# Where the added row of the first LayerNorm joins the residual: in the input stage, or on w_out's token tiles

## The chip, the cores and the metric

One core of one Trainium2 chip runs the whole kernel. The metric is the time of the execution on the device in microseconds. Three runs of the kernel before took 1259.07, 1259.10 and 1259.88 us; the median is 1259.1.

## What is computed

A decoder layer over 1024 tokens of width 1024, with 16 meta tokens ahead of them:

```
h = layer_norm(concat(meta, x), in_ln_g, in_ln_b)
z = h @ w_in + b_in                              # q, k, v, conv input, two gates
mixed = sigmoid(g_attn) * y_attn + sigmoid(g_conv) * y_conv
h = layer_norm(DEEPNORM_ALPHA * h + mixed @ w_out, ln1_g, ln1_b)
up = causal_dwconv(h @ ffn_w_up, ffn_dw, ffn_dw_b)
return layer_norm(DEEPNORM_ALPHA * h + (gelu(g) * u) @ ffn_w_down, ln2_g, ln2_b)
```

The change concerns the term `DEEPNORM_ALPHA * h` in the fourth line. With n the normalized input, it is `n * (ALPHA * in_ln_g) + ALPHA * in_ln_b`: a row that multiplies and a row that is added, the same for all tokens.

## The kernel before

All matrix products are made of float32 operands split into a high and a low part, three matmuls for one. TensorE gets them stage by stage:

- **Input stage** (0 to about 56 us): the token tiles of 128 rows are loaded, normalized without gain and shift (tiles `xn`, the last three in the arena `OB`, and `xm` for the meta tokens), turned by TensorE, scaled by gain and shift per channel and split. The first products with w_in run in between.
- **z products, attention, convolution** (to about 400 us). The convolution is a chain of 31 taps for each of four channel blocks on DVE (L669).
- **Branches and merges** (to about 510 us): for each of eight column blocks m, the projections of both branches are multiplied by their gates and added into `mixed`; the splits of w_out for the next stage are made in between, some on POOL (L276).
- **w_out rows** (about 504 to 609 us): `out_rows(i)` makes one tile of 128 tokens; the order is 3, -1, 7, 2, 6, 0, 4, 1, 5, where -1 stands for two tokens ahead. The residual tile is loaded from DRAM (`h0d`) into one half of `RT`, a part of `OB`; two products of 512 columns (three matmuls by eight blocks each) go to PSUM; DVE adds each to the residual tile (L1251, "evacuation"), takes its statistics (L1252) and normalizes the tile (L1275). TensorE turns it (L1285, `turn`), in the middle of the next row's products, and ACT writes the turned tiles with the gain (L1298). From these, operands of a Strassen-like FFN product are formed (L1197) and split (ACT L1188, DVE L1193), and the first FFN weights too (ACT L1315, DVE L1316, L1333).
- **FFN up** (609 to about 1040 us) and **FFN down** with the last norm (to the end).

`residual` writes the tile that the w_out rows load. It loads the two rows of the first norm on all partitions (`gb`), multiplies both by ALPHA (L446), and for each of the nine tiles multiplies by the first and adds the second (L450), and stores the tile to `h0d` on SP's queue. Its work stands behind the input stage in DVE's order.

The order of each engine's instructions comes from a planner: it issues what is ready in a simulated order of time, the lowest rank first (`rank(...)`). `after(a, b)` sets an order by hand without a wait. In the w_out stage DVE's order is written out so for part of the rows: `line(ins)` puts an instruction behind the last one that was given to it, and rows 0, 4, 1 and 5 (`pin = line`) give it their evacuations, statistics and normalizations, between the forming and splitting of operands. All loads go by SP's queue, which takes them in order.

Of the kernel before, what the change touches and what calls it, by code (L numbers as in the profile page):

```python
# [23 lines left out]
F = mybir.dt.float32  # L24
R = mybir.dt.float32r
AF = mybir.ActivationFunctionType
OP = mybir.AluOpType
AX = mybir.AxisListType

P = 128  # L30
D = 1024
# [17 lines left out]
ALPHA = 2.0 ** 0.25  # L49
# [15 lines left out]
RK_TURN, RK_SPLIT, RK_EVAC, RK_START, RK_QKV, RK_RESID, RK_ATT = 450, 500, 600, 1000, 10000, 20000, 30000  # L65
# [36 lines left out]
def tile_hybrid_layer(  # L102
# [3 lines left out]
    nc = tc.nc  # L106
    PSUM = bass.MemoryType.PSUM

    def dram(ap, offset, dims):
        return bass.AP(tensor=ap.tensor, offset=ap.offset + offset, ap=[list(d) for d in dims])  # L110

    def load(o, i):
        return nc.sync.dma_start(out=o, in_=i)
# [5 lines left out]
    def f32(ap):  # L119
        return ap.bitcast(F)  # L120

    def after(ins, first):

        tc.add_manual_dep(ins.ins, first.ins.name, mybir.DependencyInfo(
            mybir.DependencyClass.NoSync, mybir.DependencyReason.SCHED_ONLY), reason="order of work")

    @contextmanager
    def rank(p):

        saved = tc.cur_priority  # L130
        tc.cur_priority = p
        yield
        tc.cur_priority = saved
# [34 lines left out]
    sp = start.enter_context(tc.tile_pool(name="start", bufs=1, side="right", reuse_waits="tile"))  # L168
# [110 lines left out]
    last_fill, last_split = [], []  # L279
# [156 lines left out]
    gb = []  # L436

    def residual(n, *js):

        if not gb:  # L440
            for i in range(2):
                gb.append(sp.tile([P, D], F, name="gb", tag="x", bufs=8))
                with rank(24):
                    load(gb[i], dram(ln0_in, i * D, [[0, P], [1, D]]))
            for t in gb:
                after(nc.vector.tensor_scalar(t, t, ALPHA, None, OP.mult), first_nm)  # L446
        for j in js:
            t, lo = (xns[j], 0) if j >= 0 else (xm, 96)
            for op, t2 in zip((OP.mult, OP.add), gb):
                after(nc.vector.tensor_tensor(t[lo:], t[lo:], t2[lo:], op), last_split[n])  # L450
            load(*((h0d[2 + j * P:2 + (j + 1) * P, :], t) if j >= 0 else (h0d[0:2, :], xm[96 + U0:96 + NMETA])))

    GT = [(-1, 0, 1), (2, 3, 4), (5, 6, 7)]
# [258 lines left out]
    for q4 in range(2):  # L712
# [5 lines left out]
        for g in range(NKV):  # L718
            hi, lo = (V[:, q4 * 4:q4 * 4 + 4, g, i] for i in range(2))
# [30 lines left out]
    for h in range(NH):  # L750
        g, r = divmod(h, 4)
# [174 lines left out]
    def pin(ins):  # L926

        if pinned:
            after(ins, pinned[-1])
        pinned.append(ins)  # L930
# [85 lines left out]
    for g in range(3):  # L1016
# [5 lines left out]
    rx_p = ctx.enter_context(tc.tile_pool(name="rx", bufs=1, side="right", reuse_waits="tile"))  # L1022
    RX = rx_p.tile([P, 2112], R, name="RX")
    wo_stack = ExitStack()
    RW = wo_stack.enter_context(tc.tile_pool(name="rw", bufs=1, side="right", reuse_waits="tile")).tile(
        [P, 2048], R, name="RW")
    RT = OB[:, 0:2048]


# [3 lines left out]
    def mixed(i, k, hl):  # L1033
        t, j = MX_AT[i]
        o = j * 2048 + (k * 2 + hl) * P
        return t[:, o:o + P]
# [12 lines left out]
    def prep_wo(k, raw=None, behind=None):  # L1049
        if k < 4:  # L1050
            hi, lo = OA[:, k * 2048:k * 2048 + 1024], OA[:, k * 2048 + 1024:k * 2048 + 2048]
        elif k < 6:
            hi, lo = ((RX, RW)[k - 4][:, x:x + 1024] for x in (0, 1024))
        else:
# [15 lines left out]
    def gslot():  # L1070
        i = g_next[0]
        t, o = GS[i if i < 4 else 4 + (i - 4) % 5]
        g_next[0] += 1
        return t[:, o:o + 516].rearrange("p (i n) -> p i n", i=2)
# [3 lines left out]
    for m in range(KC):  # L1078
        hi, lo = weights([P, KC, P], lambda raw: load(raw, w_ab[m]))

        def branch(i, g, tag, bufs):
            a, b = PG[g]
            ps = pat.tile([P, 512], F, name="ps_p", tag=tag, bufs=bufs)
            rhs = (oo, conv)[i]
            product(ps[:, :b - a], [(hi[:, 4 * i + k], lo[:, 4 * i + k], rhs(k, 0, a, b), rhs(k, 1, a, b))
                                    for k in range(4)])
            return ps[:, :b - a]

        def merge(g, psa, psb):
            a, b = PG[g]  # L1090
            n = b - a
            with rank(RK_EVAC):
                t = gslot()[:, :, :n]
                ins = load(t, dram(sgd, m * P * U + a, [[U, P], [KC * P * U, 2], [1, n]]))

                ta, tb = t[:, 0], t[:, 1]
                nc.vector.scalar_tensor_tensor(ta, ta, 1.0, psa, OP.add, OP.mult)
                nc.vector.scalar_tensor_tensor(tb, tb, 1.0, psb, OP.add, OP.mult)
                nc.vector.tensor_tensor(ta, ta, tb, OP.add)
                if g == 0:  # L1100
                    nc.scalar.mul(pair[:, m, 0:2], ta[:, 0:2], 0.5)
                    nc.vector.scalar_tensor_tensor(pair[:, m, 2:4], ta[:, 0:2], 0.5, f32(pair[:, m, 0:2]),
                                                   OP.mult, OP.subtract)
                v = ta[:, n - 256:].rearrange("p (t x) -> p t x", t=2)
                h = mixed2(g, m, 0)
                last_act = nc.scalar.mul(h, v, 0.5)
                nc.vector.scalar_tensor_tensor(mixed2(g, m, 1), v, 0.5, f32(h), OP.mult, OP.subtract)
            return ins, last_act

        if m < KC - 1:  # L1110
            for g in range(4):
                last_gate, last_act = merge(g, branch(0, g, "mm", 3), branch(1, g, "t", 2))
        else:
            pa = [branch(0, g, "mm", 3) if g < 3 else branch(0, g, "s", 2) for g in range(4)]
            for g in range(4):
                last_gate, last_act = merge(g, pa[g], branch(1, g, "t", 2))
        if m in (2, 3):
            raw = (FA[:, 4112:5136], OB[:, 3072:4096])[m - 2]
            load(raw, w_out_v[m + 2])
            prep_wo(m + 2, raw, last_act)  # L1120
        if m < 4:
            early.append(FA[:, W_AT[m]:W_AT[m] + 1024])
            after(load(early[m], w_out_v[m]), last_gate)
# [104 lines left out]
    def out_rows(i, between=(), work=()):  # L1228


        n, u = (P, 2 + i * P) if i >= 0 else (2, 0)
        if n == P:
            o = r_next[0] % 2 * 1024
            r_next[0] += 1
            whole = RT[:, o:o + 1024]
            load(whole, h0d[u:u + n, :])
        else:
            whole = OB[:, 3072:4096]
        r = whole[:n]
        order = WO_ORDER if i != 5 else (0, 1, 2, 3, 6, 7, 4, 5)  # L1240
        turned = None
        st = small.tile([P, 2, 6], F, name="st")
        pin = line if i in (0, 4, 1, 5) else lambda ins: ins
        for half in range(2):
            hs = slice(half * 512, half * 512 + 512)
            ps = pat.tile([P, 512], F, name="ps_w", tag="mm", bufs=3)
            if n == P:
                last = product(ps, [(mixed(i, k, 0), mixed(i, k, 1), wo[k][0][:, hs], wo[k][1][:, hs])
                                    for k in order], turned)
                with rank(RK_TURN):  # L1250
                    pin(nc.vector.tensor_tensor(r[:, hs], ps, r[:, hs], OP.add))  # L1251
                    pin(nc.vector.bn_stats(st[:, half], r[:, hs]))  # L1252
                turned = None
                if len(between) > half:
                    turned = turn(*between[half], behind=[last])
                if half == 0:
                    for f, *x in work:
                        f(*x)
                continue

            for j, k in enumerate(order):
                nc.tensor.matmul(ps[:4], pair[:, k], wo[k][0][:, hs], start=j == 0, stop=False)
                last = nc.tensor.matmul(ps[:2], pair[:, k, 0:2], wo[k][1][:, hs], start=False, stop=j == KC - 1)
            nc.scalar.copy(whole[:4, hs], ps[:4])
        if n < P:
            q = FA[:4, 0:1024]
            load(q[0:2], h0d[0:2, :])
            nc.vector.tensor_tensor(r, r, q[0:2], OP.add)
            load(q[0:2], whole[2:4])
            nc.vector.tensor_tensor(r, r, q[0:2], OP.add)  # L1270
        with rank(RK_TURN):
            (mu, rs), = ln_stats([(r, n)], half_stats=st if n == P else None)
            for a in (512, 0) if i == 5 else (None,):
                x = r if a is None else r[:, a:a + 512]
                ins = pin(nc.vector.tensor_scalar(x, x, mu, rs, OP.subtract, OP.mult))  # L1275
        if n == P:
            load(h1d[u - 2:u - 2 + P, :], r)
        return whole, n, ins
# [194 lines left out]
    for c in range(FC):  # L1473
        V4, X, Z, Y = (pup.tile([P, 1024], F, name=n, tag=n) for n in ("pw", "px", "pz", "py"))
        passes = ((1,), (0,)) if c == 0 else ((0, 1),)
        for subs in passes:
# [3 lines left out]
            i = max(a, 2)  # L1480
# [309 lines left out]
```

## Time and profile before

| | before |
|---|---|
| median of three runs | 1259.1 us |
| the profiled execution's own time | 1259.33 us |
| its span | 1257.1 us |
| granted TensorE clock | 0.998 |
| busy: TensorE, DVE, ACT, POOL | 1246.0, 1086.6, 587.4, 54.1 us |

The profile was taken of one execution. In its rows PE is TensorE's matmuls and PEld its weight loads, DVE is VectorE, ACT ScalarE, POOL GpSimd, and SP the engine whose queue issues the loads. A row of an order of time gives start and length in us, engine, line of the kernel, operation, output and inputs, shape and count; in brackets the idle time of the engine before it and what ended it. Matmuls are pipelined and their ends are modelled, so that a full TensorE need not be at its peak.

### The profile page before, as it was taken

What the parts mean: (1) busy time and instruction counts of PE and PEld (TensorE: products, weight loads), DVE (VectorE), ACT (ScalarE), POOL (GpSimd) and SP (SyncE); (2) the same over time, 40 slices, a digit from 0 to 9 for tenths busy, and PEclk for the clock granted to TensorE, in tenths of its full rate; (3) what the DMA queues carried; (4) which work ended last, traced back from release to release, by engine and by line L of the source; (5) the groups of instructions that cost most, each with busy time, mean ns of one, the idle gap of its engine ahead of it and who ended that gap; (6) DMA issues with size and microseconds to landing.
All of it is one profiled execution on the core that took longest, in us unless ns stands there. A gap on an engine that the chain in (4) does not pass through costs nothing.

```text
span 1257.1 us, 21713 instructions
## 1 busy us (share of the span) xinstructions
PE 1246.0 (99%) x8546; PEld 1179.2 (94%) x8546; DVE 1086.6 (86%) x1859; ACT 587.4 (47%) x1057; POOL 54.1 (4%) x28
## 2 busy tenths in 40 slices
PE   9999999999999999999999999999999999999997
PEld 8999999999999999788899999999999998888886
DVE  7899989999989587648899999999999986995697
ACT  7522244545474222335565555554555554544330
POOL 0000000010112132000000000000000000000000
PEclk9999999999999999999999999999999999999999
DMA  7294733332155565222145555463464568998722
GB/s 279 73 309 104 192 95 97 106 94 81 68 141 178 155 171 140 77 75 101 68 134 185 193 210 187 184 218 117 154 230 164 203 211 318 390 328 298 249 86 84
DMA packets 96152, 212.10 MB, mean 169 GB/s; under 512 B 10787, under 2 KB 35939, under 8 KB 95922
## 3 DMA queue, kind: packets, MB, share of 16 engines
q1 hardware_dynamic: 84282, 199.64, 47.4%
q10 hardware_dynamic: 11768, 11.08, 2.7%
q8 instruction: 67, 1.10, 0.4%
q14 instruction: 35, 0.29, 0.1%
HBM read 150.29 MB, written 62.70 MB: 169 GB/s over the span
## 4 chain that ended last, share of the span: by engine, by line
PE 96%; ACT 1%; DVE 1%; DMA 0%; issue 0%; ACTq 0%; DVEq 0%; SPq 0%
PE px L1497 14%; PE py L1497 9%; PE ps_x L1635 9%; PE ps_z L305 8%; PE ps_z L301 8%; PE ps_z L306 8%; PE ps_z L1635 7%; PE pz L1497 5%; PE pw L1497 5%; PE ps_p L306 2%; PE ps_p L301 2%; PE ps_p L305 2%; PE ps_w L306 2%; PE ps_w L301 2%; PE ps_w L305 2%; PE ps_z L517 2%
## 5 line engine op out<-in xcount | busy, mean ns | idle before, releaser
L669 DVE SCALAR_TENSOR_TENSOR FA<-cin,cols,FA 128x1026 f32<-128x1026 f32 x120 | 155.2, 1305 | 0.2
L301 PE MATMUL ps_z<-RHO,whi 128*128 128x384 f32 (+2 forms) x324 | 104.7, 323 | 0.2 <-ACT FA L676 0.2
L305 PE MATMUL ps_z<-RHC,whi 128*128 128x384 f32 (+2 forms) x324 | 104.5, 323 | 0.0
L305 PE MATMUL ps_z<-RHO,whi 128*128 128x384 f32 (+2 forms) x324 | 104.0, 321 | 0.0
L306 PE MATMUL ps_z<-RHC,wlo 128*128 128x384 f32 (+2 forms) x324 | 103.7, 320 | 0.0
L301 PE MATMUL ps_z<-RHC,whi 128*128 128x384 f32 (+2 forms) x324 | 103.7, 320 | 0.0
L306 PE MATMUL ps_z<-RHO,wlo 128*128 128x384 f32 (+2 forms) x324 | 103.4, 319 | 0.0
L1316 DVE TENSOR_TENSOR RHO<-wr,RHO 128x512 fp32r<-128x512 f32 x94 | 63.6, 686 | 5.4 <-ACT RHO L1315 5.4
L1315 ACT CAST RHO<-wr 128x512 fp32r<-128x512 f32 x94 | 56.7, 620 | 24.4 <-DVE wr L1333 11.5
L273 ACT CAST whi<-wr 128x1024 fp32r<-128x1024 f32 x37 | 38.9, 1051 | 56.3 <-PE ps_z L305 31.9
L301 PEld LDWEIGHTS ps_z<-RHO,whi 128*128 128x128 f32 x324 | 60.9, 188 | 0.9 <-ACT FA L676 0.4
L305 PEld LDWEIGHTS ps_z<-RHC,whi 128*128 128x128 f32 x324 | 60.9, 188 | 0.4
L306 PEld LDWEIGHTS ps_z<-RHC,wlo 128*128 128x128 f32 x324 | 60.9, 188 | 0.2
L301 PEld LDWEIGHTS ps_z<-RHC,whi 128*128 128x128 f32 x324 | 60.9, 188 | 0.2
L306 PEld LDWEIGHTS ps_z<-RHO,wlo 128*128 128x128 f32 x324 | 61.0, 188 | 0.1
L305 PEld LDWEIGHTS ps_z<-RHO,whi 128*128 128x128 f32 x324 | 60.9, 188 | 0.1
L1333 DVE TENSOR_TENSOR wr<-wr 128x512 f32<-128x512 f32 x88 | 60.3, 685 | 0.2
L276 POOL TENSOR_TENSOR wlo<-wr,whi 128x1024 fp32r<-128x1024 f32 x17 | 42.3, 2488 | 185.3 <-ACT whi L273 175.7
L676 ACT ACTIVATE FA<-ps_z,cols 128x386 f32<-128x386 f32 (+2 forms) x48 | 26.0, 541 | 46.6 <-PE ps_z L306 39.1
L1509 ACT COPY FA<-px 128x514 f32<-128x514 f32 (+2 forms) x23 | 13.1, 571 | 68.0 <-PE px L1497 67.8
L1316 DVE TENSOR_TENSOR ws<-wr,ws 128x512 fp32r<-128x512 f32 x60 | 40.6, 686 | 4.5 <-ACT ws L1315 4.3
L1422 ACT ACTIVATE FA<-OB,cols 128x512 f32<-128x512 f32 x44 | 35.9, 816 | 14.0 <-DVE OB L1505 14.0
(467 smaller groups left out, 3567.3 us busy)
## 6 DMA issues: line engine op xcount, KB each, us to landing
wr<-in_w_up_dram SPq DMA_DIRECT2D x44, 512.0 KB, 4.6
wr<-in_w_z_dram SPq DMA_DIRECT2D x30, 512.0 KB, 4.0
fd<-FA SPq DMA_DIRECT2D x44, 256.0 KB, 2.5
OB<-in_w_down_dram SPq DMA_DIRECT2D x19, 512.0 KB, 6.2
qt<-qd SPq DMA_DIRECT2D x28, 256.0 KB, 3.7
td<-OB SPq DMA_DIRECT2D x12, 512.0 KB
sums<-fd SPq DMA_DIRECT2D x12, 512.0 KB, 4.8
sd<-sums SPq DMA_DIRECT2D x12, 512.0 KB, 2.7
```

What stands on the lines that cost most here:

```text
L273: ins = nc.scalar.copy(hi, raw)
L276: return (nc.vector if quick else nc.gpsimd).tensor_tensor(lo, raw, f32(hi), OP.subtract)
L301: ins = nc.tensor.matmul(ps, ah, bh, start=i == 0, stop=False)
L305: nc.tensor.matmul(ps, ah, bl, start=False, stop=False)
L306: last = nc.tensor.matmul(ps, al, bh, start=False, stop=i == n - 1)
L669: nc.vector.scalar_tensor_tensor(acc[c], cin[:, j:j + U], wc, acc[c], OP.mult, OP.add)
L1315: nc.scalar.copy(hi, src)
L1316: ins = nc.vector.tensor_tensor(lo, src, f32(hi), OP.subtract)
L1333: ins = nc.vector.tensor_tensor(*x)
L1422: nc.scalar.activation(t, cc[:, 2:HW], AF.Identity, bias=ffw(3, o), scale=ffw(2, o))
L1497: ins = nc.tensor.matmul(o, x[:, ks], bmat(sub, q, hl, k), start=first and k + j == 0, stop=k == 3 and j == 2, skip_group_check=not first)
L1635: nc.tensor.matmul(banks[i], l[:, ts], r[:, ws], start=first and a and x + k == 0, stop=z and x == len(ops) - 1 and k == 2, skip_group_che ...
```

## The change

The row that is added goes out of the input stage: `residual` loads only the row that multiplies, and `h0d` holds `n * ALPHA * in_ln_g`. The other row gets a tile of its own, `beta`, on the right side beside w_out's split block `RW`; it is loaded in the merges at m == 1 and multiplied by ALPHA at m == 3. In `out_rows` the tile that came from `h0d` gets `beta` added as a whole, in the order ahead of its two evacuations (for rows 0, 4, 1 and 5 by `line`). The two tokens of row -1 get it between two adds.

```diff
     def residual(n, *js):
 
         if not gb:
-            for i in range(2):
-                gb.append(sp.tile([P, D], F, name="gb", tag="x", bufs=8))
-                with rank(24):
-                    load(gb[i], dram(ln0_in, i * D, [[0, P], [1, D]]))
+            gb.append(sp.tile([P, D], F, name="gb", tag="x", bufs=8))
+            with rank(24):
+                load(gb[0], dram(ln0_in, 0, [[0, P], [1, D]]))
             for t in gb:
                 after(nc.vector.tensor_scalar(t, t, ALPHA, None, OP.mult), first_nm)
         for j in js:
             t, lo = (xns[j], 0) if j >= 0 else (xm, 96)
-            for op, t2 in zip((OP.mult, OP.add), gb):
-                after(nc.vector.tensor_tensor(t[lo:], t[lo:], t2[lo:], op), last_split[n])
+            after(nc.vector.tensor_tensor(t[lo:], t[lo:], gb[0][lo:], OP.mult), last_split[n])
             load(*((h0d[2 + j * P:2 + (j + 1) * P, :], t) if j >= 0 else (h0d[0:2, :], xm[96 + U0:96 + NMETA])))
...
-    RW = wo_stack.enter_context(tc.tile_pool(name="rw", bufs=1, side="right", reuse_waits="tile")).tile(
-        [P, 2048], R, name="RW")
+    rw_p = wo_stack.enter_context(tc.tile_pool(name="rw", bufs=1, side="right", reuse_waits="tile"))
+    RW = rw_p.tile([P, 2048], R, name="RW")
+    beta = rw_p.tile([P, D], F, name="beta")
...
+        if m == 1:
+            load(beta, dram(ln0_in, D, [[0, P], [1, D]]))
+        if m == 3:
+            with rank(RK_EVAC):
+                nc.vector.tensor_scalar(beta, beta, ALPHA, None, OP.mult)
         if m in (2, 3):
...
         pin = line if i in (0, 4, 1, 5) else lambda ins: ins
+        if n == P:
+            with rank(RK_TURN):
+                pin(nc.vector.tensor_tensor(r, r, beta, OP.add))
         for half in range(2):
...
             nc.vector.tensor_tensor(r, r, q[0:2], OP.add)
+            nc.vector.tensor_tensor(r, r, beta[0:2], OP.add)
             load(q[0:2], whole[2:4])
             nc.vector.tensor_tensor(r, r, q[0:2], OP.add)
```

## The prediction

> **What bounds the kernel now.** First the page: busy times by engine, and the shares of the chain that ended last.
>
> ```profile
> PE 1246.0 (99%) x8546; PEld 1179.2 (94%) x8546; DVE 1086.6 (86%) x1859; ACT 587.4 (47%) x1057; POOL 54.1 (4%) x28
> PE 96%; ACT 1%; DVE 1%; DMA 0%; issue 0%; ACTq 0%; DVEq 0%; SPq 0%
> ```
>
> TensorE is busy for 1246.0 of 1257.1 us, and 96% of the chain is its own matmuls. DVE, whose work is all that the change touches, is second. So the change moves the end only where it makes TensorE wait, or takes a wait away. The view of busy time by stretches (us, then for each engine busy time and instructions, clock, DMA share, GB/s) shows where TensorE is not full.
>
> ```profile
> core 0: us, PE busy (x) PEld busy (x) DVE busy (x) ACT busy (x) POOL busy (x), PEclk, DMA share, GB/s
> 0.00:20.00 20.00, 18.36 (x112) 16.74 (x113) 14.46 (x43) 13.11 (x22) 2.67 (x7) 1.00 0.89 346
> ...
> 60.00:80.00 20.00, 20.00 (x130) 20.00 (x129) 19.24 (x22) 5.00 (x8) 0.00 (x0) 1.00 0.79 261
> ...
> 370.00:400.00 30.00, 29.79 (x189) 29.59 (x188) 28.41 (x54) 18.70 (x28) 7.89 (x3) 1.00 0.44 134
> ...
> 440.00:480.00 40.00, 40.00 (x340) 40.00 (x339) 32.21 (x61) 11.38 (x24) 14.71 (x6) 1.00 0.62 162
> ...
> 580.00:600.00 20.00, 20.00 (x95) 16.64 (x94) 16.94 (x27) 11.19 (x25) 0.00 (x0) 1.00 0.22 79
> ...
> 610.00:620.00 10.00, 9.02 (x76) 8.59 (x75) 8.49 (x18) 7.00 (x17) 0.00 (x0) 1.00 0.45 156
> 620.00:640.00 20.00, 19.69 (x166) 19.29 (x166) 20.00 (x33) 14.71 (x24) 0.00 (x0) 1.00 0.16 54
> ...
> 1050.00:1257.00 207.00, 199.11 (x879) 164.54 (x877) 161.62 (x233) 74.28 (x84) 0.00 (x0) 0.99 0.68 244
> ```
>
> TensorE lacks 0.21 us in 370 to 400, 0.98 in 610 to 620 and 0.31 in 620 to 640: 1.50 us in all. With the 1.64 of the first 20 us and the 7.89 after 1050, which the change doesn't touch, that is 11.03 of the 11.1 us that it lacks in the whole span. In the stretch from which work is taken (60 to 80) TensorE is full, though DVE is full too; in the one that gets work (the w_out rows, about 504 to 609) it is full as well, and DVE is near 85% at its close. Where the change adds DVE work stand the two larger stalls, right behind the rows.
>
> **What is removed.** The view of the instructions on the tile gb (duration minimum/median/maximum in ns):
>
> ```profile
> L450 DVE TENSOR_TENSOR xn<-xn,gb x8: 1205/1216/1225, 54.7 to 70.9; 128x1024 f32<-128x1024 f32 x8
> L450 DVE TENSOR_TENSOR OB<-OB,gb x8: 1205/1206/1207, 64.1 to 76.5; 128x1024 f32<-128x1024 f32 x8
> L446 DVE TENSOR_SCALAR gb<-gb x2: 689/690/690, 50.5 to 51.1; 128x1024 f32<-128x1024 f32 x2
> L450 DVE TENSOR_TENSOR xm<-xm,gb x2: 1221/1221/1221, 53.4 to 59.3; 32x1024 f32<-32x1024 f32 x2
> ```
>
> Half of the 18 L450 go, one of the two L446, and one 512 KB load. Back to back, an L450 costs less than it lasts, as the DVE's order of time shows (start, us, instruction, idle before it):
>
> ```profile
> 64.05 2.34 DVE L450 TENSOR_TENSOR OB<-OB,gb 128x1024 f32<-128x1024 f32 x2
> 66.32 1.21 DVE L450 TENSOR_TENSOR xn<-xn,gb 128x1024 f32<-128x1024 f32 x1
> ...
> 79.55 0.48 DVE L660 SCALAR_TENSOR_TENSOR cin<-ps_z,cols,FA 128x256 f32<-128x256 f32 x1 [0.73 <-PE ps_z L306]
> ```
>
> Two take 66.32 - 64.05 = 2.27 us, so 1.14 each. Removed: 9 x 1.14 + 0.60 (the two L446 start 0.6 apart) = 10.9 us of DVE in 50 to 78. None of it is on the path: TensorE never waits here, and at 79.55 it is DVE that waits for TensorE. What moves up is DVE's own later work (key copies, then the convolution's taps), by less than 10.9 us. TensorE's matmuls in 80 to 500 are full already, so the worth is 0 to the 0.21 in 370 to 400; I take 0, the value of all the other stretches. On SP one load less is queued at the start, and the nine h0d stores leave earlier, long before the rows read them.
>
> **What is added before the rows.** The beta load on SP at m == 1 is 512 KB, as a row load is:
>
> ```profile
> OB<-h0d SPq DMA_DIRECT2D x8, 512.0 KB, 3.5
> ...
> ```
>
> Its place is that of the convolution norm's temporaries, read for the last time before the first merge is done, and nobody reads beta before m == 3. Queued behind it on SP are gate tiles and weights for later merges. Its bounds are 0 (those are fetched ahead) and 3.5 us (a merge waits out one whole transfer, and its bank with it); I take 0, since TensorE has 40.00 of 40.00 us in 440 to 480 with the DMA engines at 0.62. The ALPHA multiply at m == 3 costs 0.60 on a DVE that is idle for 40.00 - 32.21 = 7.79 us there: 0. One thing can stretch it, for a split on POOL stretches DVE work in these merges:
>
> ```profile
> 429.82 1.96 DVE L1107 SCALAR_TENSOR_TENSOR RHC<-FA,RHC 128x256 fp32r<-128x256 f32 x1
> ```
>
> ```profile
> 429.09 2.40 POOL L276 TENSOR_TENSOR wlo<-wr,whi 128x1024 fp32r<-128x1024 f32 x1 [8.96 <-ACT whi L273]
> ```
>
> This L1107 ends with POOL's split, at 431.5 to 431.8. Meeting one, the multiply could last 0.69 + 2.40 = 3.1 us, still under 7.79. [...]
>
> **What is added in the rows.** Eight adds of 1.14 us and one of 2x1024 in the meta row (1.2, as the 32-partition L450 lasts as long as the full one). All can start once the row has landed, 3.5 us after issue. Rows 3, 7, 2, 6 and 0 and the meta row have DVE idle ahead of them, of which the widest kind is this:
>
> ```profile
> 562.12 0.69 DVE L1251 TENSOR_TENSOR OB<-ps_w,OB 128x512 f32<-128x512 f32 x1 [4.92 <-PE ps_w L306]
> ```
>
> Their price is 0. Rows 4, 1 and 5 are chained by line(), each add behind all work formed before it and ahead of its row's evacuation, on a DVE that is nearly full. So the order of time there decides:
>
> ```profile
> 579.63 0.68 DVE L1251 TENSOR_TENSOR OB<-ps_w,OB 128x512 f32<-128x512 f32 x1
> ...
> 583.64 1.23 DVE L1193 TENSOR_TENSOR OC<-OB,OC 128x1024 fp32r<-128x1024 f32 x1 [1.41 <-ACT OC L1188]
> ...
> 591.52 0.69 DVE L1251 TENSOR_TENSOR OB<-ps_w,OB 128x512 f32<-128x512 f32 x1
> ...
> 597.60 0.69 DVE L1316 TENSOR_TENSOR RHO<-wr,RHO 128x512 fp32r<-128x512 f32 x1 [0.69 <-ACT RHO L1315]
> 598.21 0.68 DVE L1251 TENSOR_TENSOR OB<-ps_w,OB 128x512 f32<-128x512 f32 x1
> ...
> 600.81 0.82 DVE L1275 TENSOR_SCALAR OB<-OB,mv,sd 128x1024 f32<-128x1024 f32 x1
> ...
> 605.25 0.68 DVE L1251 TENSOR_TENSOR OB<-ps_w,OB 128x512 f32<-128x512 f32 x1
> ...
> 609.25 0.69 DVE L1251 TENSOR_TENSOR OB<-ps_w,OB 128x512 f32<-128x512 f32 x1 [1.38 <-PE ps_w L306]
> ...
> 611.86 1.00 DVE L1275 TENSOR_SCALAR OB<-OB,mv,sd 128x512 f32<-128x512 f32 x2
> ...
> 613.38 0.42 DVE L1505 TENSOR_TENSOR FA<-pz,OB 128x256 f32<-128x256 f32 x1
> ...
> 615.97 0.69 DVE L1316 TENSOR_TENSOR ws<-wr,ws 128x512 fp32r<-128x512 f32 x1 [0.98 <-ACT ws L1315]
> ```
>
> Row 4: +1.14 at 579.63; the idle 1.41 at 583.64 takes it up, provided that ACT's cast doesn't move with DVE. ACT's order of time says that it doesn't: that cast stands behind eight evacuations of transposes, these behind TensorE, and what it reads was formed before 579.63.
>
> ```profile
> 579.78 2.90 ACT L1298 ACTIVATE FA<-ps_h,cols 128x128 f32<-128x128 f32 x8 [0.25 <-DMA h1d<-OB]
> 582.53 1.08 ACT L1188 CAST OC<-OB 128x1024 fp32r<-128x1024 f32 x1
> ```
>
> Left over: 0. Row 1: +1.14 at 591.52. The 0.69 at 597.60 is no cover, since that ACT copy waits for the DVE sums before it and moves along. So the row's normalization, 600.81 + 0.82 = 601.63, now ends at 602.77. Who waits for it are row 1's transposes on TensorE:
>
> ```profile
> 602.71 1.04 PE L1285 MATMUL ps_h<-cols,OB 128*128 128x128 f32 x8
> ```
>
> They start at 602.71: TensorE waits about 0.1 us. Row 5: its own add makes the debt 2.28 at 605.25; the idle 1.38 before 609.25 leaves 0.90. The normalization (two halves of about 0.5 from 611.86) then ends at about 613.3 and 613.8. From TensorE's order of time:
>
> ```profile
> 613.29 0.60 PE L1285 MATMUL pw<-cols,OB 128*128 128x128 f32 x4
> 613.85 0.66 PE L1285 MATMUL pz<-cols,OB 128*128 128x128 f32 x4
> 615.49 1.68 PE L1497 MATMUL pw<-RHC,RHO 128*128 128x256 f32 x12 [0.98 <-ACT FA L1298]
> ```
>
> The first four transposes start on time; the other four wait for L1505, 613.38 + 0.90 + 0.42 = 614.70, and still end before 615.49, until when TensorE idles now for ACT. DVE's idle 0.98 before 615.97 takes up the last 0.90. If one of these covers were gone, its add would cost up to 1.14 us.
>
> **Sum.** 0 + 0 + 0.1: the profiled execution (1259.33 us, around a span of 1257.1) becomes 1259.4. That run lay 0.2 over the median of the runs, 1259.1; on the median the forecast is 1259.2.
>
> **The rivals.** *The covers move too (slower).* If ACT's casts behind rows 4 and 5 follow DVE, or the planner puts other DVE work into those holes, nothing is taken up and the debt at row 5's normalization is 3 x 1.14 = 3.42 us, less the slack of about 0.9 to the first transposes (612.4 to 613.29): +2.5, 1261.7; with the stalls behind it, where DVE has 20.00 of 20.00 us, the whole 3.4: 1262.6. It decides from a debt of 0.9 us on at row 5. For it speaks the full DVE of 620 to 640; against it, that ACT is 56% busy in 580 to 600 and that its cast hangs on TensorE. *The planner lays the queues anew (slower).* Issue order comes from a planner that sees 10.9 us less on DVE early, and TensorE takes its queue in order; a matmul put too early waits for DVE, at the most as long as the shift, 10.9 us; half of it gives +5, 1264. Against it: 0.21 us is all that TensorE waits from 20 to 610 now, and the shift is small beside DVE's 1086.6 us. *The relief counts (faster).* If the early relief ends the 0.21 in 370 to 400 and a new order half of the 1.29 behind the rows: -0.9, 1258.2; with all of the 1.50, 1257.6. It can't reach 0.2% of the time, 2.5 us, without touching the ends. *The change does nothing* is the forecast itself, with DVE's work moved.
>
> **How the numbers follow.** 0.2%, about what a measurement of this kernel can tell from no change, is 2.5 us. Chances: forecast, within about 0.5 us of 1259.2, 0.50; relief 0.14, of which 0.05 past 2.5 us through a new order at the ends; covers move 0.24, half of it past 2.5 us; planner 0.12, nearly all past it. So faster 0.05, same 0.71, slower 0.24. The range leaves out the planner's case and the far part of the relief, and takes in the moved covers: 1258.2 to 1262.6.
>
> **What would show it.** Right: the DVE idle of 4.92 us before row 0's evacuation shrinks by 1.1, and 1.38 before row 5's to about 0, row 5's second evacuation comes 0.9 after its product, and TensorE's idle time in 600 to 640 stays at about 1.4 us. Wrong: row 1's or row 5's transposes wait over 0.5 us for L1275, a new TensorE wait stands in 80 to 500, or DVE's idle 1.41 behind row 4 is still there.

## The result and the profile after

| | before | after |
|---|---|---|
| median, 14 runs each on the same chip | 1259.63 us (1259.07 to 1260.01) | 1262.18 us (1261.53 to 1262.65) |
| ratio of the medians | | 1.0021, 95% interval 1.0014 to 1.0028 |
| the profiled execution's own time | 1259.33 us | 1261.75 us |
| its span | 1257.1 us | 1259.5 us |

The kernel became 2.55 us slower, 0.2%. The forecast of no change did not come: each of the 14 runs lies above each of the 14 of the kernel before. The range, up to 1262.6, holds the result. In the page's busy times and chain, TensorE's work is what it was and its share of the chain fell.

```profile
PE 1246.1 (99%) x8546; PEld 1178.4 (94%) x8546; DVE 1091.0 (87%) x1859; ACT 588.6 (47%) x1057; POOL 54.7 (4%) x28
PE 93%; DVE 5%; DMA 1%; ACT 1%; issue 0%; SPq 0%; DVEq 0%
```

So the loss is waits of TensorE, and DVE stands in the chain where it stood with 1% before. The busy time by stretches (the columns as before):

```profile
60.00:80.00 20.00, 20.00 (x132) 20.00 (x132) 15.89 (x31) 5.44 (x11) 0.00 (x0) 1.00 1.02 338
...
320.00:345.00 25.00, 24.03 (x149) 22.96 (x148) 24.63 (x24) 10.00 (x23) 5.03 (x2) 1.00 0.23 77
...
370.00:400.00 30.00, 30.00 (x195) 30.00 (x195) 27.38 (x52) 19.84 (x29) 7.92 (x3) 1.00 0.40 111
...
610.00:620.00 10.00, 8.93 (x68) 8.00 (x68) 8.70 (x18) 4.78 (x13) 0.00 (x0) 1.00 0.31 108
620.00:640.00 20.00, 19.43 (x164) 19.00 (x163) 19.83 (x33) 14.40 (x24) 0.00 (x0) 1.00 0.14 45
```

DVE is relieved in 60 to 80 (19.24 before, 15.89 now), and the 0.21 us that TensorE lacked in 370 to 400 are gone. In their place TensorE lacks 0.97 us in 320 to 345, where it lacked nothing, as this row of the kernel before shows:

```profile
320.00:345.00 25.00, 25.00 (x165) 24.07 (x165) 24.67 (x39) 12.70 (x33) 2.57 (x2) 1.00 0.21 72
```

It also lacks more than before in 610 to 640. The view of waits on TensorE names what ended them (total, times, longest):

```profile
PE ps_o L866 <- DVE OB L793: 1.0, 1, 1.0
PE pw L1505 <- ACT FA L1306: 0.8, 1, 0.8
PE px L1505 <- ACT OB L1517: 0.6, 1, 0.6
...
PE ps_h L1293 <- DVE OB L1283: 0.2, 1, 0.2
```

Lines have moved by the edit: L793 is the sum of halves of an attention block (L795 before), L1250 the new add of `beta`, L1258 the evacuation (L1251 before), L1283 the normalization (L1275), L1293 the turn (L1285), L1505 the FFN's matmuls (L1497).

When the same matmul, counted from the first, starts later than in the kernel before says where the time goes: at 20 us +0.1 (a wait for the normalization L431 that is 0.8 us longer than before leaves next to nothing behind), at 320 us -0.2, from 390 to 590 us +1.2, at 608 +1.7, from 640 to the end +2.41, which is the whole difference of the spans. So half of it arises in the attention and half in the 30 us around the end of the rows.

**The attention.** First TensorE's order of time, then ACT's, then DVE's, then DVE's of the kernel before.

```profile
340.15 0.50 PE L866 MATMUL ps_o<-ph,v 128*128 128x512 f32 x1 [0.97 <-DVE OB L793]
```

```profile
333.45 0.58 ACT L792 COPY OB<-ps_o 64x512 f32<-64x512 f32 x1 [1.30 <-PE ps_o L868]
```

```profile
330.79 8.58 DVE L667 SCALAR_TENSOR_TENSOR FA<-cin,cols,FA 128x1026 f32<-128x1026 f32 x5
339.40 0.69 DVE L793 TENSOR_TENSOR OB<-OB,ps_o 64x512 f32<-64x512 f32 x1
```

```profile
334.58 0.69 DVE L795 TENSOR_TENSOR OB<-OB,ps_o 64x512 f32<-64x512 f32 x1
```

The sum of halves L793 could run at 334.03, when ACT's copy was done. It ran at 339.40, since five taps of the convolution stood ahead of it in DVE's queue, 8.58 us of them. Before, taps came one at a time between the attention's small work, and the sum ran at 334.58. DVE is no fuller there by what the change adds: nothing is added before 414 us. The early relief made the planner's order another one.

One thing more belongs to this wait. The five taps are not alike: four last 1.28 or 1.29 us, and the fifth, beside a split on POOL, 3.30.

```profile
336.07 3.30 DVE L667 SCALAR_TENSOR_TENSOR FA<-cin,cols,FA 128x1026 f32<-128x1026 f32 x1
```

```profile
335.65 2.64 POOL L276 TENSOR_TENSOR wlo<-wr,whi 128x1024 fp32r<-128x1024 f32 x1 [9.77 <-ACT whi L273]
```

Without these 2.0 us the sum would have run at about 337.4 and ended at 338.1, and TensorE began its last product ahead of L866 at 338.83. So by this estimate five taps at their usual length would not have made TensorE wait; the order and the stretched tap do it together. No run here parts the two.

**The rows.** DVE's order of time shows each add with the evacuation behind it.

```profile
561.39 1.23 DVE L1250 TENSOR_TENSOR OB<-OB,beta 128x1024 f32<-128x1024 f32 x1 [2.96 <-DMA OB<-h0d]
563.36 0.69 DVE L1258 TENSOR_TENSOR OB<-ps_w,OB 128x512 f32<-128x512 f32 x1 [0.74 <-PE ps_w L306]
...
580.87 1.22 DVE L1250 TENSOR_TENSOR OB<-OB,beta 128x1024 f32<-128x1024 f32 x1
582.19 0.69 DVE L1258 TENSOR_TENSOR OB<-ps_w,OB 128x512 f32<-128x512 f32 x1
...
584.90 1.23 DVE L1197 TENSOR_TENSOR OC<-OB,OC 128x1024 fp32r<-128x1024 f32 x1
...
603.40 0.81 DVE L1283 TENSOR_SCALAR OB<-OB,mv,sd 128x1024 f32<-128x1024 f32 x1
...
607.83 1.22 DVE L1250 TENSOR_TENSOR OB<-OB,beta 128x1024 f32<-128x1024 f32 x1
609.15 0.69 DVE L1258 TENSOR_TENSOR OB<-ps_w,OB 128x512 f32<-128x512 f32 x1
...
611.70 0.68 DVE L1258 TENSOR_TENSOR OB<-ps_w,OB 128x512 f32<-128x512 f32 x1
```

From each add to the evacuation that reads its tile it is 582.19 - 580.87 = 1.32 and 609.15 - 607.83 = 1.32 us, not the 1.14 of two independent adds. Row 0's is covered: the idle 4.92 became 2.96 + 0.74. Row 4's is covered too: the L1197 at 584.90 starts without idle time, 1.26 later than before on a kernel that is 1.24 late by then. Row 1's and row 5's are not, as TensorE's order of time shows.

```profile
604.36 1.07 PE L1293 MATMUL ps_h<-cols,OB 128*128 128x128 f32 x8 [0.25 <-DVE OB L1283]
...
610.73 1.58 PE L1505 MATMUL px<-OC,RHO 128*128 128x256 f32 x12
612.44 1.65 PE L1505 MATMUL pz<-OC,RHO 128*128 128x256 f32 x12
...
624.10 1.69 PE L1505 MATMUL px<-RHC,RHO 128*128 128x258 f32 x12 [0.57 <-ACT OB L1517]
```

Row 1's turn comes 1.65 later than before's 602.71, so it lost 0.41 by waiting for the normalization that ends at 604.21. The second FFN group comes 1.71 us behind the first; in the kernel before it was 1.41 (609.05 to 610.46). It takes over the PSUM bank of row 5's second evacuation, which ends at 611.70 + 0.68 = 612.38; the view of that line names the group's first weight load as waiting 0.3 us for it. So 0.30 is lost. The rest, up to 1.2 for the rows, is about 0.1 around row 5's transposes and 0.3 before the px group at 624.10, which waited 0.31 before and waits 0.57 now. By the chain that ended last, this group waits behind a load of weights, which begins when a split on DVE is done. The split comes 2.23 later than the 615.97 of the kernel before, since the ACT cast that it waits for comes as much later:

```profile
618.20 0.69 DVE L1324 TENSOR_TENSOR ws<-wr,ws 128x512 fp32r<-128x512 f32 x1 [0.77 <-ACT ws L1323]
```

### The profile page after: what moved, and what is told of

It reads as the page before. It is cut to its first block, busy times and chain, and to the rows that moved or that the text cites. A ratio compares the mean times of both kernels' runs of the same rounds, so it can differ in the third digit from the quotient of the medians.

```text
span 1259.5 us, 21712 instructions
## 1 busy us (share of the span) xinstructions
PE 1246.1 (99%) x8546; PEld 1178.4 (94%) x8546; DVE 1091.0 (87%) x1859; ACT 588.6 (47%) x1057; POOL 54.7 (4%) x28
## 4 chain that ended last, share of the span: by engine, by line
PE 93%; DVE 5%; DMA 1%; ACT 1%; issue 0%; SPq 0%; DVEq 0%
PE px L1505 14%; PE py L1505 9%; PE ps_x L1643 9%; PE ps_z L305 8%; PE ps_z L301 8%; PE ps_z L306 8%; PE ps_z L1643 7%; PE pz L1505 5%; PE pw L1505 5%; PE ps_p L306 2%; PE ps_p L301 2%; PE ps_p L305 2%; PE ps_z L515 2%; PE ps_w L301 1%; PE ps_w L306 1%; PE ps_w L305 1%
## 5 line engine op out<-in xcount | busy, mean ns | idle before, releaser
L667 DVE SCALAR_TENSOR_TENSOR FA<-cin,cols,FA 128x1026 f32<-128x1026 f32 x120 | 158.0, 1329 | 0.6
L1324 DVE TENSOR_TENSOR RHO<-wr,RHO 128x512 fp32r<-128x512 f32 x94 | 63.3, 683 | 5.3 <-ACT RHO L1323 5.2
L1341 DVE TENSOR_TENSOR wr<-wr 128x512 f32<-128x512 f32 x88 | 59.9, 681 | 0.2
L276 POOL TENSOR_TENSOR wlo<-wr,whi 128x1024 fp32r<-128x1024 f32 x17 | 42.1, 2474 | 179.9 <-ACT whi L273 171.0
L1324 DVE TENSOR_TENSOR ws<-wr,ws 128x512 fp32r<-128x512 f32 x60 | 40.5, 684 | 4.3 <-ACT ws L1323 4.2
```

Source lines behind the costliest of these rows:

```text
L276: return (nc.vector if quick else nc.gpsimd).tensor_tensor(lo, raw, f32(hi), OP.subtract)
L667: nc.vector.scalar_tensor_tensor(acc[c], cin[:, j:j + U], wc, acc[c], OP.mult, OP.add)
L1324: ins = nc.vector.tensor_tensor(lo, src, f32(hi), OP.subtract)
L1341: ins = nc.vector.tensor_tensor(*x)
```

## The experiments

Theory A: the two halves of the change cost on their own, each about 1.2 us, the early one through the planner's other order in the attention, the late one through the adds chained ahead of rows 1 and 5. Its rival B: all of it comes from the adds that were put late. A third cause, that work on POOL stretches the DVE work beside it, was tried for the rows by itself; for the tap at 336, 3.30 us long in place of 1.28, it was not. Ratios are to the kernel before, run on the same chip, with 95% intervals.

**Only the early half.**

```diff
-            load(beta, dram(ln0_in, D, [[0, P], [1, D]]))
...
-                nc.vector.tensor_scalar(beta, beta, ALPHA, None, OP.mult)
...
-                pin(nc.vector.tensor_tensor(r, r, beta, OP.add))
...
-            nc.vector.tensor_tensor(r, r, beta[0:2], OP.add)
```

> Only the early half of the change: the input stage multiplies and doesn't add, and nothing is added later (the added row is left out of the result). Theory A (the 2.4 us have two sources: 1.2 from DVE's new order in the attention, where TensorE waits for a bank behind five convolution taps, and 1.2 from the adds in the w_out rows): 1.2 us over the kernel before, with TensorE's wait of about 1 us before a product of the attention near 339 us, and the rows as before. Rival B (all comes from the rows' adds, and the attention's wait is made up for elsewhere): within 0.3 us of before.

Measured: 1260.32 us, ratio 1.0009 (1.0001 to 1.0018), +1.06 us; each of its 11 runs lies above each of the 33 of the kernel before. Its view of waits has the attention's wait, in full, and none of the rows':

```profile
PE ps_o L866 <- DVE OB L793: 1.0, 1, 1.0
```

B is false: with no late add at all (the added row is left out of the result), taking work from DVE between 50 and 78 us costs 1 us at 339.

**Only the late half.**

```diff
 # residual() as in the kernel before
             for op, t2 in zip((OP.mult, OP.add), gb):
...
+                pin(nc.vector.tensor_tensor(r, r, beta, OP.add))
```

The row is thus added twice.

> Only the late half: the input stage is the one of the kernel before, and the row is loaded, multiplied and added in the rows as well (so it is added twice in the result). Theory A: 1.2 us over the kernel before, all of it between 600 and 625 us, and no wait in the attention. Rival B: 2.4 us.

Measured: 1261.75 us, ratio 1.0020 (1.0011 to 1.0029), +2.49 us. The wait in the attention is gone, as A said, but the rows cost twice what A gave them. TensorE's order of time and the stretches say why.

```profile
616.64 0.66 PE L1295 MATMUL pz<-cols,OB 128*128 128x128 f32 x4 [1.54 <-DVE FA L1515]
618.09 2.52 PE L1507 MATMUL pw<-RHC,RHO 128*128 128x256 f32 x12 [0.79 <-ACT FA L1308]
620.40 2.31 PE L1507 MATMUL py<-OC,ws 128*128 128x256 f32 x12
```

```profile
618.00:620.00 2.00, 1.91 (x11) 1.91 (x12) 0.92 (x2) 2.00 (x7) 0.00 (x0) 0.65 0.73 234
620.00:622.00 2.00, 2.00 (x11) 2.00 (x11) 1.97 (x4) 1.63 (x3) 0.00 (x0) 0.50 0.23 94
```

Two things that theory A lacked: row 5's second transposes wait 1.54 us for L1515 (0.18 in the changed kernel), and behind that the granted clock falls to 0.5 for about 3.4 us, so that two groups of twelve matmuls last 2.52 and 2.31 us (1.63 and 1.52 at a clock of 1.00, in the run below with only rows 1 and 5 late). By the mean clock not every run had that drop: it is 0.998 or 0.999 in six of the eleven, 1261.11 to 1261.75 us, and 0.997 in the other five, 1262.34 to 1262.76, of which the profiled one is one.

**Row 1 and row 5 alone, in two forms.** First these two as before and the other seven late; then these two late and the others as before.

```diff
+    EARLY_ADD = (1, 5)            # second form: all others, and the two tokens
...                                # both rows are loaded again
-            after(nc.vector.tensor_tensor(t[lo:], t[lo:], gb[0][lo:], OP.mult), last_split[n])
+            for op, t2 in zip((OP.mult, OP.add), gb if j in EARLY_ADD else gb[:1]):
+                after(nc.vector.tensor_tensor(t[lo:], t[lo:], t2[lo:], op), last_split[n])
...
-        if n == P:
+        if n == P and i not in EARLY_ADD:
```

> The change for all tiles but those of rows 1 and 5, which get the row added in the input stage. If the debt of DVE in the w_out rows is that of the adds of rows 1 and 5 alone (row 4's taken up by the idle time of 1.41 us behind it, the others' by idle time ahead of their evacuations), the rows cost 0 and TensorE's waits from 600 to 640 are those of the kernel before; what is left over before is the attention's 1.2 us or less. If row 4's add counts too, the turn of row 1 waits still, and 0.3 to 1 us stay in the rows.

Measured: 1259.80 us, ratio 1.0005 (0.9996 to 1.0014). Row 1's turn is not a wait any more, and the two waits behind the rows are 0.98 and 0.28 us (0.98 and 0.31 before): in the rows seven late adds are free. What is left arises in the attention, waits of 0.4 and 0.2 us for DVE at 339 and 345.

> The other way round: only rows 1 and 5 get the row late, all others in the input stage. If rows 1 and 5 make the debt: the rows cost about 1.2 us, as in the whole change, with nearly no change of the attention (two of nine adds less there), so 1.2 us over before. If the debt is that of all the rows' adds together: under 0.6 us.

Measured: 1262.20 us, ratio 1.0021 (1.0012 to 1.0030), +2.94 us. That is more than twice what was expected, though the attention is as before. With the run ahead of it, it says that the late adds' cost is that of these two; how large it is hangs on the order. Its runs fall into two groups by mean clock: 1260.96 to 1261.51 at 0.998, and 1261.99 to 1262.86 at 0.997. The profile is of the first group; in it the groups of matmuls are not stretched, and the wait of row 5's second transposes is the same as in the run ahead. TensorE's rows, then DVE's:

```profile
616.43 0.66 PE L1295 MATMUL pz<-cols,OB 128*128 128x128 f32 x4 [1.50 <-DVE FA L1515]
617.88 1.63 PE L1507 MATMUL pw<-RHC,RHO 128*128 128x256 f32 x12 [0.80 <-ACT FA L1308]
```

```profile
614.03 0.69 DVE L1326 TENSOR_TENSOR ws<-wr,ws 128x512 fp32r<-128x512 f32 x1
614.75 0.69 DVE L1343 TENSOR_TENSOR wr<-wr 128x512 f32<-128x512 f32 x1
615.36 0.69 DVE L1326 TENSOR_TENSOR ws<-wr,ws 128x512 fp32r<-128x512 f32 x1
615.96 0.42 DVE L1515 TENSOR_TENSOR FA<-pz,OB 128x256 f32<-128x256 f32 x1
```

Here the planner put three instructions on weights between the normalization and L1515; in the changed kernel only one L1324 stands there. In the rows the same two adds thus cost 1.2 us in the changed kernel's order, 1.6 in this one (its matmuls are 0.07 us late at 590 and 1.64 at 640), and 1.5 more in the runs at a mean clock of 0.997.

**Row 1 alone, row 5 alone.**

```diff
+    EARLY_ADD = (-1, 0, 2, 3, 4, 5, 6, 7)     # and (-1, 0, 1, 2, 3, 4, 6, 7)
```

> Only row 1 gets the row late. By the account of debt and cover: its add costs DVE 1.33 us, row 1's turn waits 0.4 us, and the idle 1.38 before row 5's second evacuation takes up the rest: +0.4 us over the kernel before. If the two rows' costs just add up: about half of what rows 1 and 5 cost together, 1.5 us.

Measured: 1259.62 us, ratio 1.0003 (0.9994 to 1.0012), +0.38 us. In the profile the turn comes 0.4 late, as worked out, and 0.3 of it is won back at the px group, which waits no more; the rest is inside the interval.

> Only row 5 gets the row late. By the account of debt and cover: 1.33 us of debt against 1.38 of idle time ahead of its second evacuation: 0 us, TensorE's waits from 600 to 625 as in the kernel before. If the two rows' costs just add up: 1.5 us.

Measured: 1263.55 us, ratio 1.0033 (1.0021 to 1.0046). In the rows every start is late by the same 5.8 us, so row 5's add alone costs nothing, as the debt says. But the 5.8 us arise before 100 us. TensorE's order of time, DVE's and the stretches:

```profile
82.51 0.70 PE L301 MATMUL ps_z<-RHO,whi 128*128 128x400 f32 x1 [2.83 <-DVE cin L661]
```

```profile
80.68 1.22 DVE L276 TENSOR_TENSOR wlo<-wr,whi 128x1024 fp32r<-128x1024 f32 x1 [3.83 <-ACT whi L273]
```

```profile
82.00:88.00 6.00, 5.49 (x16) 5.44 (x17) 5.67 (x16) 0.00 (x0) 0.00 (x0) 0.50 1.03 402
```

With one row's work moved, the input stage got an order in which an evacuation (L661) stands behind a split of weights (L276) whose input isn't ready; TensorE waits 2.8 us, and the clock is at 0.5 until about 88.6 us.

**The taps put behind the sum.** The changed kernel, with the taps from the 25th on of the last channel block set behind the last block's first sum of halves.

```diff
+                    if c == 3 and j >= 25:
+                        after(ins, halves[-2])
```

> The whole change, and by hand one order on DVE: the taps 25 to 30 of the last convolution block stand behind the last block's first add of halves, which in the whole change waited 5.4 us in DVE's queue (ready at 334.0, run at 339.4) behind five taps while TensorE stood still for its bank. If the early half's cost is that order of DVE's queue: TensorE's wait near 339 is gone and the time is 1.1 us under the whole change, 1261.1. If the cost is something else (POOL's split that stretches a tap, or the early work as such): 0 to 0.3 us.

Measured: 1261.34 us, ratio 1.0017 (1.0008 to 1.0026), 2.10 us over the kernel before on its chip, where the changed kernel was 2.55 over: 0.45 us won, between the two forecasts. The wait for L793 is gone, as the first forecast said; the rows are as in the changed kernel; and the small wait at 382, which the changed kernel had lost, is back and larger:

```profile
PE ps_z L301 <- ACT FA L676: 0.5, 1, 0.5
```

So the order on DVE does end the wait for the sum, but half of what that wins is lost again 40 us later. The order by hand also takes the tap that POOL stretches out of the sum's way, so it doesn't tell the two apart.

**Rows 1 and 5 on POOL.**

```diff
+                if i in (1, 5):
+                    nc.gpsimd.tensor_tensor(r, r, beta, OP.add)
+                else:
+                    pin(nc.vector.tensor_tensor(r, r, beta, OP.add))
```

> The whole change with the adds of rows 1 and 5 on POOL, which has nothing else to do there; all others on DVE. If it is DVE's issue time that costs in the rows: TensorE's waits from 600 to 625 are those of the kernel before, and 1.2 us go. If POOL's add and DVE's splits and differences from SBUF shut each other out (the stretched DVE instructions beside POOL's splits speak for it): each POOL add of about 2.4 us delays DVE by up to as much, and the rows cost as much as before or more, 0 to +1 us against the whole change.

Measured: 1261.74 us, ratio 1.0020 (1.0011 to 1.0028). Nothing is won; in the profile the rows cost 1.15 us, in the changed kernel 1.2. POOL's add and what runs on DVE beside it:

```profile
597.76 2.40 POOL L1251 TENSOR_TENSOR OB<-OB,beta 128x1024 f32<-128x1024 f32 x1 [7.30 <-DVE wr L1344]
```

```profile
597.07 4.36 DVE L1344 TENSOR_TENSOR wr<-wr 128x512 f32<-128x512 f32 x3
```

Three L1344 last 4.36 us; in the changed kernel, where nothing ran on POOL, the same three (L1341) took 2.15. DVE lost 2.2 us to an add that it no longer made, and row 1's turn waits 1.2 us.

**Both repairs.** Rows 1 and 5 early, and the taps put behind the sum.

> Both repairs together: rows 1 and 5 get the added row in the input stage as in the kernel before, the other seven on w_out's tiles, and the taps from the 25th on of the last channel block are put behind the last attention block's first sum of halves. If the two causes (the debt at rows 1 and 5; DVE's order in the attention) are the whole of the loss, no wait is left in the rows but those of before (1.15 and 0.44 us at 615 and 621), and the waits of 0.57 and 0.34 us at 339 and 345 go: 1259.3 us, the time of before within 0.5. If taps that are put off make TensorE wait at the gates instead, as the 0.71 us at 382 did with all nine rows late, about 0.5 stays there: 1259.7. If there is a third cause, the time stays above 1260.5.

Measured: 1263.39 us, ratio 1.0034 (1.0022 to 1.0046). The waits at 339 and 345 (0.41 and 0.17 us in the view of the run with rows 1 and 5 early; the expectation's gaps are all some 0.15 larger than the waits in the rows shown here) are gone and the rows are as before, but a third cause came up. DVE's order of time, then TensorE's:

```profile
426.11 0.69 DVE L1127 TENSOR_SCALAR beta<-beta 128x1024 f32<-128x1024 f32 x1 [7.53 <-DMA beta<-in_ln_dram]
426.71 0.42 DVE L1104 SCALAR_TENSOR_TENSOR FA<-FA,ps_p 128x258 f32<-128x258 f32 x1
```

```profile
427.19 0.39 PE L301 MATMUL ps_p<-OC,whi 128*128 128x256 f32 x1 [3.68 <-DVE FA L1104]
```

The planner moves the ALPHA multiply from the merge m == 3 to the middle of the first; there it waits for beta's load, which with the DMA engines full (a share of 1.04 in 421.97 to 425.39) takes 8.6 us from issue to landing, and holds the evacuations of the first merge. In the changed kernel the multiply stands ahead of the first merge too and waits 5.2 us for the load, but DVE is done with the gates earlier and TensorE never waits.

**The multiply at m == 6.**

```diff
-        if m == 3:
+        if m == 6:
```

> The kernel with both repairs, but beta is multiplied by ALPHA at m == 6 and not at m == 3. In the run before this one TensorE waited 3.85 us at 423 for a merge evacuation (L1104) that stood in DVE's queue behind that multiply, and the multiply waited 7.53 us for beta's load. If the late load is the third cause, the wait at 423 goes and DVE never waits for beta: 1259.5 us, with at most one small wait in the attention or at the gates. If the merge is late for another reason (the gates, 4 us later than without the tap order), the wait stays and the time is over 1262.

Measured: 1264.19 us, ratio 1.0040 (1.0026 to 1.0054). A miss that says something: the multiply did not move, since its place is the planner's choice and not that of the loop, and it waited 8.2 us for the load:

```profile
PE ps_p L301 <- DVE FA L1104: 4.4, 1, 4.4
```

Behind this wait the granted clock is 0.5 for 3.4 us, which it was not in the profile of the run ahead.

**The multiply pinned.**

```diff
 # last_lo holds the merges' last split so far on DVE, here that of m == 3
-                nc.vector.tensor_scalar(beta, beta, ALPHA, None, OP.mult)
+                after(nc.vector.tensor_scalar(beta, beta, ALPHA, None, OP.mult), last_lo[0])
```

> Again both repairs, and the ALPHA multiply now put by hand behind the last split of the fourth merge on DVE: at m == 6 alone the planner still put it between the first two evacuations of the first merge, where it waited 8.2 us for beta's load. If that wait is the third cause, TensorE's wait of 3.9 to 4.5 us at 423 goes, the clock stays at 1.0, and nothing is left but small waits: 1259.4 us, the time of before within 0.5. If the gates, which run some 4 us later with the tap order, make the merge late, the wait stays: over 1262.

Measured: 1259.01 us (1258.80 to 1259.53), ratio 0.9998 (0.9989 to 1.0007). The wait is gone, and of TensorE's waits behind the first 20 us the view of waits lists one, the larger of the two that the kernel before has behind the rows:

```profile
PE pw L1513 <- ACT FA L1314: 1.0, 1, 1.0
```

With two rows left in the input stage and DVE's order mended in two places, what is left of the change costs nothing, and gains nothing: 0.19 us under the kernel before, inside the interval. That is the forecast's "relief 0", reached only when nothing new is made to wait. The multiply now stands at 466 us beside a split on POOL and lasts 2.88 us, under the 3.1 that the prediction gave as its bound, and nobody waits for it.

## Why the prediction was right or wrong

**Held.** TensorE is the bound, and the time changed only by its waits. The relief in 50 to 78 is worth nothing by itself. The rows 3, -1, 7, 2, 6 and 0 cost nothing (the run with only rows 1 and 5 early), and row 4's add is taken up by the idle 1.41, which is gone. The 1.38 before row 5's second evacuation is gone too, and that evacuation comes 0.77 us later against TensorE than before, where 0.9 was forecast. A split on POOL does stretch DVE work beside it, as the tap of 3.30 us at 336 shows; in the rows, where POOL has 0.00 us in 580 to 600, nothing was stretched until an add was put there.

**Wrong: the early relief's other side, taken as 0.** The sum said that the worth was 0 to 0.21 and left the loss to the rival "the planner lays the queues anew", half of the shift, +5. The mechanism came, at a quarter of that size: +1.22 in the profile, +1.06 in the run with the early half alone. The error was to price the removed work by what DVE saved and the new order only as a mishap. The prediction had said that a new TensorE wait in 80 to 500 would prove it wrong; it stands at 339.

**Wrong: the rows' term, 0.1 for what measured 1.2.** Three parts were mis-sized. The add was priced back to back at 1.14; the evacuation reads what it writes, and it takes 1.32. So row 1's normalization ended 1.34 late by DVE alone (604.21 - 1.24 - 601.63), 0.20 more than forecast, and the turn started 0.15 behind that end: it waited 0.41, not 0.1 (0.40 in the profile with row 1 alone). The debt at row 5 was thus 1.32 + 1.32 - 1.38 = 1.26 before TensorE's own delay, not 0.90. And the hand-over of a PSUM bank from row 5's second evacuation to the second FFN group, 0.30 us, was not in the sum at all: only the transposes had been looked at. Last, the idle 0.98 before 615.97 was to take up what was left, and 0.77 of it is still there: the ACT cast that it waits for moved along, and with it the load behind it, which is the 0.3 before the px group. "The covers move too" had that cast in view, but its price was for all three adds uncovered. The covers of 1.41 and 1.38 held, so only this part of it came.

**Right by luck.** The range holds the result, but not for its reason: its upper end, 1262.6, was set for a debt of 3.4 us in the rows, and half of the 2.55 us came from the attention by the planner's new order, a case that the range left out. The multiply of beta was priced at 0 on a DVE that is idle for 7.79 us in the merges. It cost 0, but it was put into the first merge, where it waits for a load; the first run with both repairs paid 3.7 us for that. The bound of 3.5 us for the load was for a merge that waits for its own data; what came is a wait in DVE's queue for data that nobody needs for another 90 us.

## What to carry to other kernels

Where a planner sets the order of the queues, work that is taken away is a change of order, and its price is read from the waits that the new order makes, not from the time saved. An operation that can run early will be put early: where its input is a late load, bind it behind the work that must not wait for it. And a sum of debts along a chained queue needs every consumer behind each link, the next owner of a PSUM bank included, and the dependent cost of an operation (1.32 us here), not its cost beside independent ones (1.14).

## What the hardware showed that was not expected

The granted clock fell by half behind waits shorter than the drop that followed. With only the late half it was 0.5 for about 3.4 us from 618.6 on; in the 3.4 us ahead of that TensorE had two waits, of 1.54 and 0.79 us, and worked in between. With only row 5 late it was 0.5 from about 81.8 to 88.6, and the one wait was 2.83 us.

How idle TensorE was ahead of a drop can be read from the traces. The clock's changes lie whole multiples of 3.413 us apart in them. From the first change to the drop at the kernel's end it is 1245.865 us before and 1249.278 after, 3.413 more, which makes 365 and 366 such steps; with only the late half it is 614.399 us from the first change to the drop, 180 steps; with only row 5 late 75.093 us, 22 steps. Cut by that step, the stretches just ahead of a drop are these, with only the early half (the drop at the kernel's end), only the late half and only row 5 late. With the multiply at m == 6 TensorE was busy for 0.08 us of such a stretch. The last row is the idlest stretch of all traces with no drop behind it, with both repairs.

```profile
1249.47:1252.88 3.41, 1.36 (x6) 0.78 (x5) 3.27 (x7) 0.29 (x1) 0.00 (x0) 1.00 0.41 154
615.20:618.61 3.41, 1.18 (x8) 0.94 (x9) 3.19 (x6) 2.87 (x9) 0.00 (x0) 1.00 0.81 301
78.36:81.78 3.41, 1.32 (x12) 1.12 (x10) 1.09 (x1) 1.04 (x1) 0.00 (x0) 1.00 1.03 421
421.97:425.39 3.42, 1.53 (x13) 1.32 (x12) 0.00 (x0) 0.00 (x0) 0.00 (x0) 1.00 1.04 416
```

TensorE was busy for 1.36 us or less ahead of every drop in the thirteen traces, and for 1.53 in the last row: a stretch that was idle for 60% had a drop behind it, one that was idle for 55% had none. So in these traces it seems to count how a wait lies across the step. The wait of 3.68 us with both repairs lay across two stretches, of which each was idle for 1.9 us or less, and its profile has no drop. The kernel with rows 1 and 5 late had the waits of 1.50 and 0.80 us in two stretches in its profile, and no drop either; the median of its runs at a mean clock of 0.997, which have no trace, lies 1.5 us above that of the others. One and the same wait thus cost here itself, or itself and, it seems, 1.5 us more.
